# A first stage with a written order of products, and other engines for the carry weights, the latent squares and the last attention block

## The chip, the core and the metric

The kernel runs on one core of a Trainium2 chip, in one launch. A core has TensorE (PE) with its weight loads (PEld), VectorE (DVE), ScalarE (ACT), GpSimd (POOL), and SyncE (SP), which issues the transfers from the chip's main memory. Each engine runs its own list of instructions in order and waits at semaphores for the others. The metric is the device time in microseconds (us) of one execution, as the median of several runs.

## What is computed

A trunk of two layers over 512 latent tokens and 256 context tokens of width 1024, in float32. Layer 0 mixes tokens with a bidirectional mLSTM, layer 1 with windowed attention; a squared-ReLU MLP follows each. Every part is modulated by shifts, scales and gates from the condition vectors. Cut from the reference:

```
for i in range(DEPTH):                          # DEPTH = 2
    mod_l = split(silu(c) @ ada_w[i] + ada_b[i], 6)       # latent
    mod_c = split(silu(c_ctx) @ ada_w[i] + ada_b[i], 6)   # context
    u  = rms_norm(h,  norm_mix[i]) * (1 + mod_l[1]) + mod_l[0]
    uc = rms_norm(hc, norm_mix[i]) * (1 + mod_c[1]) + mod_c[0]
    y, yc = mlstm(uc, u, ...) if i == 0 else swa(uc, u, ...)
    h = h + mod_l[2] * y
    h = h + mod_l[5] * (square(relu(modulated_norm(h) @ w1)) @ w2)
    ...                                         # hc likewise, in layer 0
return rms_norm(h, final_norm)
# mlstm: q, k, v, o, gates = split(u @ w_in);  chunks of 128 tokens
#   b = cumsum(log_f);  m_t = max(max(d), b + m0);  carry_w = exp(b + m0 - m_t)
#   num = (exp(d - m_t) * (q k^T)) v + carry_w * (q C0);  h = num / max(|den|, exp(-m_t))
# swa: softmax over 384 latent keys, 256 context keys and a sink; o @ w_out
```

## The kernel before, in words

Activations lie transposed: 8 tiles (k) of 128 features, each 512 latent ("L") and 256 context ("C") tokens wide. A float32 product is made of three products of parts with fewer bits: data and weights are split into a high part (uH, whi) and a rest (uL, wlo), and `mm3` (L94 to L98) issues high by high, high by rest and rest by high. Weights come by `unit`: a load, a cast to whi on ACT (L887) and a subtraction to wlo on DVE (L888), in `split`.

The build places instructions on each engine in an order of its own, from dependencies and its estimates of durations; those marked `keep_in_program_order` (through `keep`, or through the flag `pin` in `split`) stay as written.

**First stage** (`layer0_mix`, L354 to L444). x is loaded (`load_x`); ACT squares each tile (L376), DVE adds pairs (L380), PE sums them with a ones vector (L382). DVE makes rs (L385), POOL raises it to the power -1/2 (rc, L387), PE transposes rc to rows (L321), and copies put 1/rms in rb. For each k, `cols` makes the modulation: two 512 KB tiles adaw (L204), eight products to the rows tile arow (L212), a copy on ACT, two products to fm (L221), then amix and mod on DVE (L223, L225). Per k, L417 to L420 make uH and uL for both groups, and `dense` multiplies them with three weights: m = 0 is wg (the gates), m = 1 and 2 are wqk (q and k of the first head pair). That is 8 x 3 x 2 x 3 = 144 products into the six accumulators acc.

**Gates** (`gates`). From acc of wg come scans and maxima on DVE for 8 heads in two directions, on tiles of 40 rows by 768 tokens: t1, t2, and, split in a high and a low half, ast (L652, L653) and cst (L658, L659), the carry weights; the low halves are subtracted on POOL. PE transposes t1 and t2, ACT copies them to tok1 and tok2 (L670, L675). `ogate(0, ...)` gives the output gate's products of the first head pair and is told to split its two weights on POOL. `core` of a head pair makes kp (k scaled by tok1, L764) and the carry products (L751), while a generator `fill` hands out products of the next head pair.

**End of the first MLP** (`ffn0`). `back_out` adds each output tile to hL (L1144); `norm_add` (L283 to L295) squares the finished tile on ACT and adds it to ssL. For m = 1 to 5 the add runs on POOL, for m = 6 and 7 on DVE. `keys_begin` (L1468 to L1481) then makes layer 1's key and value products (pj); between them it calls two hooks for the latent group: `norm_rc` (the sums of ssL by PE, L308, then rs and rc) after part (0, 1) of its last tile, and `norm_group` (`norm_bc`, L321, then `norm_u`, which makes layer 1's uH and uL) after part (1, 0).

**End of the attention** (`layer1_mix`, `weigh`). 16 blocks (g, j); the last product of a block leaves av; ACT copies its two halves to yt and yb (L1846, L1847), POOL adds them into yT (L1849). `split_half` splits yT for the output projection, whose last group's first half of tokens (`pa`, names "A") is laid between the blocks, and whose second half ("B") follows.

## Time and profile before

| | |
|---|---|
| runs | 1549.05, 1553.58, 1553.87 us |
| median | 1553.58 us |
| profiled execution, its own time | 1551.29 us |
| span of the profiled execution | 1549.4 us |
| mean granted TensorE clock | 0.992 |
| PE's largest group (L96 mm 128x512) | 496 products, 189.4 us |

The span runs from the first to the last instruction in the trace; the profiled execution's time contains it. "L382 <- DVE sq L380: 7.4, 1, 7.4" reads: PE at L382 waited for the tile sq, made by DVE at L380; 7.4 us in all, once, the longest 7.4. A row of the timeline has the start, the duration, engine, line, operation, tiles and shapes, and in brackets the wait that ended at its start. A row of the windows has the stretch, its length, PE's busy time and products, the granted clock (1.00 is full), the busy share of the DMA engines, and GB/s.

### The profile page before, as it was taken

The numbers are of one execution on the slowest core, as the hardware profiler recorded it, in microseconds if no ns is written. First come the engines' busy times: TensorE is split into PE (matmuls) and PEld (weight loads), VectorE is DVE, ScalarE is ACT, GpSimd is POOL, SyncE is SP. The second block draws the span as 40 slices with busy tenths as digits, with TensorE's granted clock in tenths as the row PEclk, the third lists the DMA queues.
The fourth block names the chain that finished last, engine by engine and source line by source line (L and its number), as shares of the span: only waits on it lengthen the run. The fifth ranks groups of instructions, "written<-read, shape, count | busy, mean of one in ns | idle before, by whom it ended". The sixth has DMA issues, their size and how long they took to land.

```text
span 1549.4 us, 23838 instructions
## 1 busy us (share of the span) xinstructions
PE 1509.6 (97%) x9110; PEld 1355.9 (88%) x9110; DVE 1127.1 (73%) x2084; ACT 740.2 (48%) x1501; POOL 326.5 (21%) x318
## 2 busy tenths in 40 slices
PE   6999999999999999999999999999999999999998
PEld 4778888878889999999999999888887988888886
DVE  3684657488797888767676667778888875757697
ACT  4533343344573332524424355666666665545454
POOL 0322111113203222232224221243443100000000
PEclk8999999999999999999999999999999999999999
DMA  8422323234231343343443422011111424150321
GB/s 316 139 83 69 125 82 118 73 116 150 74 110 42 120 139 124 125 146 125 148 145 100 150 69 66 32 34 42 42 41 43 177 83 149 41 163 28 109 69 55
DMA packets 47848, 157.27 MB, mean 102 GB/s; under 512 B 5327, under 2 KB 8911, under 8 KB 47607
## 3 DMA queue, kind: packets, MB, share of 16 engines
q1 hardware_dynamic: 46560, 154.25, 30.3%
q8 instruction: 72, 1.18, 0.3%
q10 hardware_dynamic: 1175, 1.51, 0.3%
q14 instruction: 41, 0.34, 0.1%
HBM read 153.64 MB, written 2.10 MB: 101 GB/s over the span
## 4 chain that ended last, share of the span: by engine, by line
PE 79%; DVE 6%; issue 4%; ACT 4%; POOL 3%; DMA 1%; POOLq 0%; DVEq 0%; ACTq 0%
PE mm L96 17%; PE mm L97 16%; PE mm L98 16%; PE p L98 2%; PE p L97 2%; PE p L96 2%; PE pt L1825 2%; PE pj L96 1%; PE pj L97 1%; PE pj L98 1%; PE at L843 1%; DVE adap L262 1%; PE av L1840 1%; ACT whi L887 1%; DVE wlo L888 1%
## 5 line engine op out<-in xcount | busy, mean ns | idle before, releaser
L888 DVE TENSOR_TENSOR wlo<-raw,whi 128x1024 fp32r<-128x1024 f32 (+2 forms) x152 | 179.6, 1186 | 82.3 <-ACT whi L887 80.6
L887 ACT CAST whi<-raw 128x1024 fp32r<-128x1024 f32 (+2 forms) x155 | 154.0, 999 | 141.9 <-PE mm L97 77.4
L96 PE MATMUL mm<-uH,whi 128*128 128x512 f32 (+1 forms) x496 | 189.4, 386 | 0.0
L97 PE MATMUL mm<-uL,whi 128*128 128x512 f32 (+1 forms) x496 | 186.7, 378 | 0.7 <-DVE uL L332 0.4
L98 PE MATMUL mm<-uH,wlo 128*128 128x512 f32 (+1 forms) x496 | 186.9, 378 | 0.0
L262 DVE SCALAR_TENSOR_TENSOR adap<-raw,crow 128x1024 bf16<-128x1024 f32 x128 | 165.8, 1295 | 19.9 <-DMA raw<-ada 19.1
L96 PE MATMUL mm<-h,whi 128*128 128x384 f32 x512 | 172.9, 338 | 1.9 <-ACT h L887 1.9
L97 PE MATMUL mm<-h,whi 128*128 128x384 f32 x512 | 172.6, 337 | 0.5 <-DVE h L888 0.5
L98 PE MATMUL mm<-h,wlo 128*128 128x384 f32 x512 | 172.1, 336 | 0.0
L887 ACT CAST whi<-sum 128x512 fp32r<-128x512 f32 (+1 forms) x42 | 31.9, 761 | 165.8 <-PE mm L97 75.9
L98 PEld LDWEIGHTS mm<-uH,wlo 128*128 128x128 f32 x496 | 93.4, 188 | 17.9 <-issue 0.9
L97 PEld LDWEIGHTS mm<-uL,whi 128*128 128x128 f32 x496 | 93.6, 189 | 16.4 <-DVE uL L489 0.7
L96 PEld LDWEIGHTS mm<-uH,whi 128*128 128x128 f32 x496 | 92.9, 189 | 15.6 <-issue 0.3
L96 PEld LDWEIGHTS mm<-h,whi 128*128 128x128 f32 x512 | 96.1, 188 | 2.8 <-ACT h L887 2.8
L97 PEld LDWEIGHTS mm<-h,whi 128*128 128x128 f32 x512 | 96.1, 188 | 1.5 <-DVE h L888 1.4
L98 PEld LDWEIGHTS mm<-h,wlo 128*128 128x128 f32 x512 | 96.1, 188 | 0.0
L888 DVE TENSOR_TENSOR wlo<-wb,whi 128x1024 fp32r<-128x1024 f32 x49 | 59.2, 1221 | 35.9 <-ACT whi L887 35.8
L888 DVE TENSOR_TENSOR h<-r,h 128x384 fp32r<-128x384 f32 (+2 forms) x100 | 56.4, 568 | 34.1 <-ACT h L887 33.8
L887 ACT CAST whi<-wb 128x1024 fp32r<-128x1024 f32 x49 | 51.6, 1054 | 60.9 <-PE mm L97 27.1
L1809 POOL TENSOR_SCALAR e<-e,den 128x512 f32<-128x512 f32 (+1 forms) x64 | 49.0, 779 | 135.1 <-DVE den L1807 86.9
L98 PE MATMUL p<-t,wlo 128*128 128x384 f32 x224 | 75.4, 337 | 0.5 <-DVE wlo L888 0.5
L97 PE MATMUL p<-t,whi 128*128 128x384 f32 x224 | 75.2, 336 | 0.0
(401 smaller groups left out, 4180.0 us busy)
## 6 DMA issues: line engine op xcount, KB each, us to landing
raw<-ada SPq DMA_DIRECT2D x80, 512.0 KB, 3.6
raw<-w SPq DMA_DIRECT2D x64, 512.0 KB, 3.5
raw<-w2a SPq DMA_DIRECT2D x32, 512.0 KB, 3.5
wb<-w2b SPq DMA_DIRECT2D x28, 512.0 KB, 4.2
adaw<-ada SPq DMA_DIRECT2D x16, 512.0 KB, 7.7
hL<-xT SPq DMA_DIRECT2D x16, 256.0 KB, 3.5
raw<-wqk SPq DMA_DIRECT2D x8, 512.0 KB, 4.0
raw<-wv SPq DMA_DIRECT2D x8, 512.0 KB, 3.5
```

The lines of the kernel that those rows point to most:

```text
L96: mm(out=out, lhsT=ah, rhs=bh, start=start, stop=False)
L97: mm(out=out, lhsT=ah, rhs=bl, start=False, stop=False)
L98: mm(out=out, lhsT=al, rhs=bh, start=False, stop=stop)
L262: self.tc.keep_in_program_order(nc.vector.scalar_tensor_tensor(out=pr, in0=w, scalar=0.5, in1=self.crow[:, v, :], op0=ALU.mult, op1=ALU.mu ...
L843: mm(out=o[hh][:, i * VW:(i + 1) * VW], lhsT=pw[g, d, hh][:, i, :], rhs=v[:, 3 * g + i, hh, :], start=False, stop=i == 2)
L887: keep(self.nc.scalar.copy(out=hi, in_=src))
L888: keep((eng or self.nc.vector).tensor_tensor(out=lo, in0=src, in1=hi.bitcast(F32), op=ALU.subtract))
L1809: nc.gpsimd.tensor_scalar(out=out[ii][:, :W], in0=out[ii][:, :W], scalar1=den[:, ii:ii + 1], scalar2=1.0, op0=ALU.mult, op1=ALU.mult)
L1825: nc.tensor.transpose(out=pt[:, i * P:(i + 1) * P], in_=ps_[i][:, n * P:(n + 1) * P], identity=self.ident)
L1840: mm(out=o, lhsT=vv, rhs=ph, start=n == 0, stop=False)
```

## The change

`mm3`, `ada_rows` and `ada_cols` issue their products through a new `matmul`, which keeps the written order while `pin_mm` is set. In the first stage it is set, and the order is written out: the modulation is cut into `rows` (eight products and the copy) and `cols` (two products and the DVE rows), the splits of wg and the first wqk stand ahead of the norm, the third split after the first products of k = 1, and wg is loaded ahead of the first adaw pair. Every second context square is made by DVE. In the gates, DVE takes the subtraction of cst's low half and the splits of the first output gate's weights; the splits of the first step of the core are pinned. In `back_out` the adds of latent tiles 4 and 5 move from POOL to DVE; the hooks of `keys_begin` move to the parts (0, 3) and (1, 1), and the sums of `norm_rc` are pinned there. In the last attention block yb's copy and both adds run on DVE, and the last three parts of `pa` are issued after the second `split_half` instead of ahead of the last products.

```diff
@@ -92,10 +92,15 @@
     def mm3(self, out, ah, al, bh, bl, start, stop):
-        mm = self.nc.tensor.matmul
+        mm = self.matmul
...
         mm(out=out, lhsT=al, rhs=bh, start=False, stop=stop)
+    def matmul(self, **kw):
+        i = self.nc.tensor.matmul(**kw)
+        return self.tc.keep_in_program_order(i) if self.pin_mm else i
@@ -209,17 +214,15 @@
             for c in range(4):
-                self.nc.tensor.matmul(out=ps[32 * c:32 * c + 32], lhsT=self.cond[:, 4 * hf + c, :],
-                                      rhs=ws[hf][:, c * 256:(c + 1) * 256], start=hf == 0, stop=hf == 1)
-    def ada_cols(self, pool, ps, fm, i):
+                self.matmul(out=ps[32 * c:32 * c + 32], lhsT=self.cond[:, 4 * hf + c, :],
+                            rhs=ws[hf][:, c * 256:(c + 1) * 256], start=hf == 0, stop=hf == 1)
+    def ada_cols(self, rows, fm, i):
...
         nc = self.nc
-        rows = pool.tile([P, 256], F32, name="rows", tag="rows", bufs=2)
-        nc.scalar.copy(out=rows, in_=ps)
         for s in range(2):
-            nc.tensor.matmul(out=fm[:, 4 * i + 2 * s:4 * i + 2 * s + 2], lhsT=rows[:, s * P:(s + 1) * P], rhs=self.sel,
-                             start=True, stop=True)
+            self.matmul(out=fm[:, 4 * i + 2 * s:4 * i + 2 * s + 2], lhsT=rows[:, s * P:(s + 1) * P], rhs=self.sel,
+                        start=True, stop=True)
@@ -367,20 +370,55 @@
             self.load_x(g)
-        aw = [self.ada_load(pool, 0)]
+        raw, w = [], []
+        def load(i):
+            r = self.ring.tile([P, D], F32, name="raw", tag="raw", bufs=self.nraw)
+            n = srcs[i].shape[1]
+            nc.sync.dma_start(out=r[:, :n], in_=srcs[i])
+            raw.append(r[:, :n])
+        def parts(i):
+            w.append([self.ring.tile([P, D], F32R, name=t, tag=t, bufs=self.nsplit)[:, :raw[i].shape[1]]
+                      for t in ("whi", "wlo")])
+            self.pin = True
+            self.split(raw[i], *w[i])
+            self.pin = False
+        aw = []
+        for i in range(3):
+            load(i)
+            aw += [self.ada_load(pool, j) for j in ((0,), (1, 2), (3,))[i]]
...
         ps = self.at.tile([P, 512], F32, name="at", tag="at")
+        self.pin_mm = True
...
                 sq = pool.tile([P, n], F32, name="sq0", tag=f"sq{g}", bufs=4)
-                nc.scalar.activation(out=sq, in_=hs[kt], func=AF.Square)
+                if g == "C" and kt % 2:
+                    nc.vector.tensor_tensor(out=sq, in0=hs[kt], in1=hs[kt], op=ALU.mult)
+                else:
+                    nc.scalar.activation(out=sq, in_=hs[kt], func=AF.Square)
...
                 for j in range(n // P):
-                    nc.tensor.matmul(out=ps[:, j0 + j:j0 + j + 1], lhsT=sq[:, j * P:(j + 1) * P], rhs=self.ones,
-                                     start=kt == 1 and j0 + j == 0, stop=kt == KT - 1 and j0 + j == NCH - 1)
+                    self.matmul(out=ps[:, j0 + j:j0 + j + 1], lhsT=sq[:, j * P:(j + 1) * P], rhs=self.ones,
+                                start=kt == 1 and j0 + j == 0, stop=kt == KT - 1 and j0 + j == NCH - 1)
+        parts(0)
+        parts(1)
+        fm = self.at.tile([P, 512], F32, name="fm", tag="at")
+        rws = {}
+        def rows(i):
+            ps = self.at.tile([P, 512], F32, name="arow", tag="at")[:, :256]
+            self.ada_rows(ps, aw[i])
+            rws[i] = pool.tile([P, 256], F32, name="rows", tag="rows", bufs=2)
+            nc.scalar.copy(out=rws[i], in_=ps)
+        def cols(i):
+            self.ada_cols(rws.pop(i), fm, i)
+        rows(0)
@@ -388,29 +426,11 @@
             (nc.vector.tensor_copy if j0 else nc.scalar.copy)(out=rb[g], in_=bc)
-        fm = self.at.tile([P, 512], F32, name="fm", tag="at")
...
         acc["C"] = [c0[:, :NCX], c12[:, :NCX], c12[:, NCX:]]
-        w = []
-        def cols(i):
-            ps = self.at.tile([P, 512], F32, name="arow", tag="at")[:, :256]
-            self.ada_rows(ps, aw[i])
-            self.ada_cols(pool, ps, fm, i)
-        def dense(g, m, k):
-            sl = slice(k * P, (k + 1) * P)
-            alone = g == "L" or m == 0
-            self.mm3(acc[g][m], w[m][0][:, sl], w[m][1][:, sl], *xs[g](k), k == 0 and (alone or m == 1),
-                     k == KT - 1 and (alone or m == 2))
-        cols(0)
-        for i in range(1, 3):
-            w.append(self.unit(srcs[i - 1]))
-            aw.append(self.ada_load(pool, i))
-            cols(i)
-        w.append(self.unit(srcs[2]))
-        for i in range(KT):
+        def modulate(i):
@@ -419,12 +439,43 @@
                                                op1=ALU.subtract)
-            if i + 3 < KT:
-                aw.append(self.ada_load(pool, i + 3))
-                cols(i + 3)
-            for m in range(3):
+        def dense(k, *ms):
+            sl = slice(k * P, (k + 1) * P)
+            for m in ms:
                 for g in "CL":
-                    dense(g, m, i)
+                    alone = g == "L" or m == 0
+                    self.mm3(acc[g][m], w[m][0][:, sl], w[m][1][:, sl], *xs[g](k), k == 0 and (alone or m == 1),
+                             k == KT - 1 and (alone or m == 2))
+        cols(0)
+        modulate(0)
+        rows(1)
+        dense(0, 0)
+        cols(1)
+        modulate(1)
+        dense(0, 1)
+        rows(2)
+        dense(1, 0)
+        parts(2)
+        cols(2)
+        modulate(2)
+        dense(1, 1)
+        dense(0, 2)
+        rows(3)
+        dense(1, 2)
+        cols(3)
+        modulate(3)
+        for i in range(2, KT):
+            if i + 2 < KT:
+                aw += [self.ada_load(pool, j) for j in range(len(aw), min(KT, i + 4))]
+                rows(i + 2)
+            dense(i, 0, 1)
+            if i + 2 < KT:
+                cols(i + 2)
+                modulate(i + 2)
+            dense(i, 2)
+        self.pin_mm = False
@@ -446,11 +497,14 @@
             self.new_es(0)
-            so = self.ogate(0, xs, nc.gpsimd)
+            so = self.ogate(0, xs, nc.vector)
...
                 pass
+            self.pin = True
+            next(so)
+            self.pin = False
@@ -465,9 +519,11 @@
                         fill = self.out_early(yu)
-                    for n in core:
+                    for i, n in enumerate(core):
+                        self.pin = p + i == 0
...
                             next(fill, None)
+                    self.pin = False
@@ -656,7 +712,7 @@
             cp(out=cst[R], in_=az)
-            nc.gpsimd.tensor_tensor(out=cst[64:104], in0=az, in1=cst[R].bitcast(F32), op=ALU.subtract)
+            nc.vector.tensor_tensor(out=cst[64:104], in0=az, in1=cst[R].bitcast(F32), op=ALU.subtract)
@@ -1145,7 +1201,7 @@
                 g = "LC"[t]
-                self.norm_add(self.st, g, m, self.hview(g, m), nc.vector if m > 5 else None)
+                self.norm_add(self.st, g, m, self.hview(g, m), nc.vector if m > (5 if t else 3) else None)
@@ -1475,7 +1531,7 @@
                     self.proj_part(self.wkv[pr], j, self.rows_of(u), 256, i, t[:, 256 * pr:256 * pr + 256])
-                    if j == 4 and (pr, i) in ((0, 1), (1, 0)):
+                    if j == 4 and (pr, i) in ((0, 3), (1, 1)):
@@ -1603,7 +1659,7 @@
                         pa = self.out_part(3, ys, pt, "pt", "A", st3)
-                        parts = [f for i in range(4) for f in (parts[i], pa[i])] + pa[4:]
+                        parts = [f for i in range(4) for f in (parts[i], pa[i])] + pa[4:5]
@@ -1612,7 +1668,10 @@
                             pass
-            self.split_half(ys[3], y3, 1)
+                self.split_half(ys[3], y3, 1)
+                for f in pa[5:]:
+                    for _ in f():
+                        pass
@@ -1843,10 +1902,11 @@
             yb = sw.tile([DH, 512], F32, name="yb", tag="sp", bufs=4)
+            last = g * 4 + j == 15
             nc.scalar.copy(out=yt, in_=o[0:DH, :])
-            nc.scalar.copy(out=yb, in_=o[DH:P, :])
+            (nc.vector.tensor_copy if last else nc.scalar.copy)(out=yb, in_=o[DH:P, :])
             for i in range(2):
-                nc.gpsimd.tensor_tensor(out=ys[g][i * DH:(i + 1) * DH, :, j * P:(j + 1) * P],
+                (nc.vector if last else nc.gpsimd).tensor_tensor(out=ys[g][i * DH:(i + 1) * DH, :, j * P:(j + 1) * P],
@@ -1873,7 +1933,7 @@
             rc, st = [], self.st
-            return [lambda: rc.append(self.norm_rc(st, g)),
+            return [lambda: rc.append(self.norm_rc(st, g, tc.keep_in_program_order)),
```

PE's list in the first stage, before, from the transposes of rc on; arow and fm are the modulation's tiles, sm and rows the copied row, acc the accumulators:

```order
L321 MATMUL at<-ident,rc_232 128x128 x6
L212 MATMUL arow<-adaw,cond 32x256 x8
L221 MATMUL fm<-sm,rows 128x2 x2
L212 MATMUL arow<-adaw,cond 32x256 x4
L96 MATMUL acc<-uH_112,whi 128x512
L212 MATMUL arow<-adaw,cond 32x256 x4
L97 MATMUL acc<-uL_113,whi 128x512
L98 MATMUL acc<-uH_112,wlo 128x512
L221 MATMUL fm<-sm,rows 128x2 x2
```

The same place after the change; all these products now go through the helper's line L102:

```order
L102 MATMUL arow<-adaw,cond 32x256 x4
L324 MATMUL at<-ident,rc_270 128x128 x6
L102 MATMUL arow<-adaw,cond 32x256 x4
L102 MATMUL fm<-sm,rows 128x2 x2
L102 MATMUL arow<-adaw,cond 32x256 x8
L102 MATMUL acc<-uC_104,whi 128x256 x2
L102 MATMUL acc<-uC_104,wlo 128x256
L102 MATMUL acc<-uH_112,whi 128x512
L102 MATMUL acc<-uL_113,whi 128x512
L102 MATMUL acc<-uH_112,wlo 128x512
L102 MATMUL fm<-sm,rows 128x2 x2
```

Half of the first arow now stands ahead of the transposes, and the second arow whole, not in two halves around a latent product, ahead of the first products, which begin with those of the context (uC).

DVE's list in the gates, before, from the cast of ast's high half to kp; ast and cst are the split pairs, adap a sum of modulation rows for later layers:

```order
L652 CAST ast<-aa 40x768
L656 TENSOR_TENSOR b<-aa,m_661 40x768
L661 TENSOR_TENSOR aa<-t_658,ae 40x768
L658 CAST cst<-b 40x768
L888 TENSOR_TENSOR wlo<-raw,whi 128x1024
L262 SCALAR_TENSOR_TENSOR adap,mod_81<-raw,crow 128x1024 x2
L888 TENSOR_TENSOR wlo<-raw,whi 128x1024
L764 TENSOR_TENSOR kp<-at,tok_646 128x384 x4
```

The same place after:

```order
L708 CAST ast<-aa 40x768
L712 TENSOR_TENSOR b<-aa,m_661 40x768
L717 TENSOR_TENSOR aa<-t_658,ae 40x768
L714 CAST cst<-b 40x768
L715 TENSOR_TENSOR cst<-b,cst 40x768
L944 TENSOR_TENSOR wlo<-raw,whi 128x1024
L820 TENSOR_TENSOR kp<-at,tok_646 128x384 x4
```

The subtraction of cst and one split of an output gate weight now stand between cst's cast and kp; the two adap rows and a second split have left.

DVE's list at the end of the first MLP, before; hL is the latent stream, uC the context's modulated tile, wlo the rest of a weight, rs what follows PE's sums of ssL:

```order
L1144 SCALAR_TENSOR_TENSOR hL_3522<-mm,mod_81,hL_3522 128x384
L888 TENSOR_TENSOR wlo<-raw,whi 128x1024
L1144 SCALAR_TENSOR_TENSOR hL_4110<-mm,mod_81,hL_4110 128x384
L1144 SCALAR_TENSOR_TENSOR hL_4121<-mm,mod_81,hL_4121 128x384
L888 TENSOR_TENSOR wlo<-raw,whi 128x1024
L295 TENSOR_TENSOR ssL<-ssL,sq 128x512 x2
L311 TENSOR_SCALAR rs<-at 128x4
```

The same place after:

```order
L298 TENSOR_TENSOR ssL<-ssL,sq 128x512
L1200 SCALAR_TENSOR_TENSOR hL_3522<-mm,mod_81,hL_3522 128x384
L944 TENSOR_TENSOR wlo<-raw,whi 128x1024
L1200 SCALAR_TENSOR_TENSOR hL_4110<-mm,mod_81,hL_4110 128x384
L298 TENSOR_TENSOR ssL<-ssL,sq 128x512
L1200 SCALAR_TENSOR_TENSOR hL_4121<-mm,mod_81,hL_4121 128x384
L298 TENSOR_TENSOR ssL<-ssL,sq 128x512
L944 TENSOR_TENSOR wlo<-raw,whi 128x1024
L298 TENSOR_TENSOR ssL<-ssL,sq 128x512
L314 TENSOR_SCALAR rs<-at 128x4
```

Two more adds to ssL stand on DVE, and the second split shown, which stood ahead of both adds, now stands behind three of the four.

More of the change, by code (lines that the diff above doesn't have):

```diff
@@ L63, in __init__ @@
         self.ada_cap = None
-        self.pin = False
+        self.pin = self.pin_mm = False
         self.ada_due = 0.0
```

## The prediction

> **What bounds the kernel now.** The page comes first: the PE row and the span.
>
> ```profile
> span 1549.4 us, 23838 instructions
> PE 1509.6 (97%) x9110; PEld 1355.9 (88%) x9110; DVE 1127.1 (73%) x2084; ACT 740.2 (48%) x1501; POOL 326.5 (21%) x318
> ```
>
> PE is idle for 1549.4 - 1509.6 = 39.8 us. A change that removes no product can win from that idle time, from products run at a low granted clock, and from nothing else. The list of what PE waited for says where the idle time lies.
>
> ```profile
> PE at L382 <- DVE sq L380: 7.4, 1, 7.4
> PE at L308 <- DVE ssL L295: 2.1, 1, 2.1
> PE acc L96 <- ACT uH L419: 2.0, 2, 1.7
> PE mm L96 <- ACT y L1655: 2.0, 1, 2.0
> PE at L751 <- DVE kp L764: 1.8, 2, 1.1
> PE at L751 <- ACT tok L670: 1.7, 1, 1.7
> ```
>
> The first row is the load of x and stays. The other five are in the four places that the diff touches: the first stage (L419), the gates' start of the mLSTM (L670, L764), the latent squares at the end of the first MLP (L295), and the end of the attention (L1655). The table of windows then shows the granted clock (the column after PE busy) at two of them.
>
> ```profile
> 23.20:26.54 3.34, 1.18 (x13) 0.98 1.02 408
> 26.54:36.70 10.16, 9.92 (x41) 0.50 0.75 280
> 36.70:70.00 33.30, 33.12 (x236) 1.00 0.36 128
> 940.60:948.00 7.40, 7.11 (x35) 0.54 0.16 65
> ```
>
> After a thin stretch (1.18 us of work in 3.34) the first stage runs 10.2 us at half clock, then 33.3 us at full clock without idle time, up to its last product. The same follows the stall before 940.54. So an idle microsecond in these two places costs more than itself.
>
> The profiled execution took 1551.29 us, 1.9 more than its span; the sum goes against it. The three timed runs have their median 2.3 above it (1549.05 to 1553.87).
>
> **First stage.** Nothing is removed; it is an order. The rows that set it:
>
> ```profile
> 18.32 1.35 POOL L387 TENSOR_TENSOR rc<-rs,mhalf 128x6 f32<-128x6 f32 x1 [15.09 <-DVE rs L385]
> 21.19 1.94 PE L212 MATMUL arow<-adaw,cond 128*32 128x256 f32 x16
> 24.26 0.28 DVE L223 TENSOR_SCALAR amix<-fm,ab,sm 128x2 f32<-128x2 f32 x1 [3.40 <-PE fm L221]
> 27.18 0.74 DVE L420 SCALAR_TENSOR_TENSOR uL<-hL,mod,uH 128x512 fp32r<-128x512 f32 x1
> 35.64 0.63 PE L98 MATMUL acc<-uH,wlo 128*128 128x512 f32 x1
> 36.07 0.63 PE L97 MATMUL acc<-uL,whi 128*128 128x512 f32 x1
> 43.42 0.39 PE L96 MATMUL acc<-uH,whi 128*128 128x512 f32 x1
> 43.66 0.39 PE L97 MATMUL acc<-uL,whi 128*128 128x512 f32 x1
> 44.12 0.28 PE L96 MATMUL acc<-uC,whi 128*128 128x256 f32 x1
> 44.24 0.27 PE L97 MATMUL acc<-uC,whi 128*128 128x256 f32 x1
> 44.44 0.64 PE L212 MATMUL arow<-adaw,cond 128*32 128x256 f32 x8
> 45.01 0.38 PE L98 MATMUL acc<-uC,wlo 128*128 128x256 f32 x1
> ```
>
> From start to start, a 512-wide product takes 0.24 us (43.42 to 43.66; at half clock 0.43, 35.64 to 36.07) and a 256-wide one 0.12, so the six products of one (k, m) take 1.06. Half an arow takes 0.57 (44.44 to 45.01); with the slower product behind it I reckon 1.33 for a whole one, and 0.48 for the fm pair. Both are estimates; they are checked on the old stage: of its 144 products 133 remain at 36.70 (the 41 rows of the window are 24 of arow, 6 of fm and 11 products), 61 of them wide: 14.6 + 72 x 0.12 = 23.3, and five arow in halves (1.52) with fm 10.0, together 33.3 as measured.
>
> The new order from the same rows. Half of arow 0 moves into the wait for POOL's rc, so the second half alone stands behind the transposes: 1.0 earlier; the squares now shared with DVE give 0.1, as PE's own cold products pace them. The first amix comes at 23.2 instead of 24.26. The chain amix to the end of uL keeps its length, 27.92 - 24.26 = 3.66: uL ends at 26.9. arow 1 stands whole ahead of the first products (23.2 to 24.3) instead of in two halves around one that waits until 26.54. The last two wide products of (0, 0) follow uL at half clock, to 27.7; fm 1 to 28.3 (estimated at somewhat over its 0.48), the six of (0, 1) to 30.2. If the clock is back by then, the rest is arow 2 1.33, (1, 0) 1.06, fm 2 0.48, (1, 1) 1.06: 34.1. Then (0, 2) waits for the third weight's low half, which DVE now makes inside modulate(2): about 35.1, its last products 35.9. arow 3 and (1, 2) reach 38.3; fm 3, four more arow and fm, and six k of 3.18 are 26.8: the stage ends at 65.1 instead of 70.0. One window more at half clock (3.4 us) takes back 1.7. I take **4.5**. The bounds: 1.0 (two windows more, and a wait for loads) and 6.5 (never cold).
>
> The loads are the cover that could go. wg is now issued ahead of ada's first pair.
>
> ```profile
> 10.73 0.91 SPq L204 DMA_DIRECT2D adaw<-ada  x2
> adaw<-ada SPq DMA_DIRECT2D x2, 512.0 KB, 5.6
> ```
>
> The two loads of that pair, issued from 10.73 on, landed 5.6 later on the median, so the first at about 16.3. With one 512 KB load ahead, 1.3 us at the 408 GB/s of the window's row, it lands at 17.6; PE wants it when its last square sum is done, a little before rc's start at 18.32. If it is late, the transposes behind it in PE's queue are late with it, by 1.3 at most; that is within the lower bound.
>
> **Gates.** DVE instead of POOL subtracts cst (L659) and splits the first head pair's wo.
>
> ```profile
> 77.29 0.95 DVE L625 SCALAR_TENSOR_TENSOR gz<-gz,aa 40x768 f32<-40x768 f32 x1 [3.94 <-ACT aa L623]
> 88.09 0.55 DVE L652 CAST ast<-aa 40x768 fp32r<-40x768 f32 x1
> 91.29 3.18 POOL L888 TENSOR_TENSOR wlo<-raw,whi 128x1024 fp32r<-128x1024 f32 x1
> 92.12 2.76 DVE L658 CAST cst<-b 40x768 fp32r<-40x768 f32 x1
> 95.03 2.79 POOL L659 TENSOR_TENSOR cst<-b,cst 40x768 fp32r<-40x768 f32 x1 [0.56 <-DVE cst L658]
> 101.23 1.94 DVE L764 TENSOR_TENSOR kp<-at,tok 128x384 f32<-128x384 f32 x4
> ```
>
> The cast of cst takes 2.76 beside POOL's split and 0.55 alone. Then the cast ends at about 92.7 and the subtraction (0.95, as the 40x768 of L625) at 93.6 instead of 97.82. The Trainium skill, "SBUF — State Buffer", section "Who interferes with whom", has the two engines share a port pair by a lock, so that the second waits until the first is done; the cast did end 0.4 behind the split (94.88 against 94.47), so the trace agrees, and it gives the sum nothing further.
>
> Two of the splits now on DVE (1.26 each, as the row 937.83 below has a split alone) fit into the 3.94 before gz. The third stands before the kp rows: queued behind it are kp, then PE's fourth carry product. With tok copied ahead of the casts on ACT, the split ends at about 100.0, and kp starts there instead of 101.23 (two adap rows have left its way). The wait for tok (1.7) goes, and of the wait for kp the smaller of its two times, 1.8 - 1.1 = 0.7; the longer lies at a later head pair. The sum is 2.4; I take **2.0**, bounds 0.5 (a third split that comes late) and 2.4.
>
> **Latent squares.** For m = 4 and 5 the add moves from POOL to DVE, and the sum's products go behind nine more pj products.
>
> ```profile
> 934.48 3.52 POOL L295 TENSOR_TENSOR ssL<-ssL,sq 128x512 f32<-128x512 f32 x2 [2.86 <-ACT sq L291]
> 934.85 2.00 DVE L888 TENSOR_TENSOR wlo<-raw,whi 128x1024 fp32r<-128x1024 f32 x1
> 937.83 1.26 DVE L888 TENSOR_TENSOR wlo<-raw,whi 128x1024 fp32r<-128x1024 f32 x1
> 939.01 1.47 DVE L295 TENSOR_TENSOR ssL<-ssL,sq 128x512 f32<-128x512 f32 x2
> 940.54 1.28 PE L308 MATMUL at<-ones,ssL 128*128 128x1 f32 x8 [2.05 <-DVE ssL L295]
> ```
>
> DVE was the engine that came last here, not POOL: POOL was done at 938.0, DVE's last add at 940.48. DVE gets two adds more (2 x 0.74 = 1.5) and one split is 0.8 shorter, so its last add ends about 0.7 **later**, at 941.2, and the last split, now behind three of the four adds, at 940.6. PE then stalls for that split and again for the sum, some 2 us as before, but with nine products (1.1) more behind it. Net 0.3 to 1.1 if the clock falls as before. The half-clock stretch (7.4 us, 46% lost, 3.4 us) may stay out, since the stall falls into other windows. I take **0.8**; bounds -1.0 (the last split later still) and 3.0 (no half clock, less a wait that then shows in the uL chain).
>
> The Trainium skill, "TensorE: Matmul & The Clock Gate", section "Why this matters for your kernels", wants PE's gaps below about 3 us for the clock to stay. By that rule a stall of 2.05 us would cost only itself and this term would be 0.8 with no upper end; the 0.54 of the window's row speaks against it.
>
> **End of the attention.**
>
> ```profile
> 1193.98 0.58 ACT L1846 COPY yt<-av 64x512 f32<-64x512 f32 x1 [0.41 <-PE av L1841]
> 1194.58 0.58 ACT L1847 COPY yb<-av 64x512 f32<-64x512 f32 x1
> 1195.24 1.58 POOL L1849 TENSOR_TENSOR yT<-yt,yb 64x256 f32<-64x256 f32 x2 [0.77 <-ACT yb L1847]
> ```
>
> From the last av product to y's cast (L1655) there are two copies, then two adds on POOL. On two engines the copies lie side by side (0.6 less). The adds on DVE have no row here; they lie between 0.74 for both (an add twice as wide takes 0.74, the row at 939.01) and POOL's 1.58, and I take 0.8, as DVE's row is the nearer one: 0.8 less. That is 1.4 of a wait of 2.0. The last av products also move six narrow products (0.7) ahead, which adds to the cover; against it two DVE rows (nAuH, hL) now stand before y's low half, and DVE may still be at one when yb is wanted, some 0.5 each at most. I take **1.2**, bounds 0.6 and 2.0.
>
> **Sum.** 4.5 + 2.0 + 0.8 + 1.2 = 8.5: 1551.3 - 8.5 = 1542.8. Placing it halfway from the profiled run to the median adds 1.2: **1544.0**.
>
> **Rivals.**
> - *The clock comes back early*: full clock in the first stage from the start and no half-clock stretch at the squares: 6.5 + 2.0 + 3.0 + 1.2 = 12.7, so 1539.8. For it: the written order has no gap of several us. Against: the first products still wait for uL.
> - *The first stage's gain is given back*: the gates' chain (DVE scans, ACT's tables) starts from the same products, but if a load or the crow rows hold it, PE waits where it did not. Then 4.0 is left: 1548.5. Against: DVE had 3.94 to spare before gz, more than the two splits that are put there.
> - *The change does little*: the lower bounds of all four, 1.1 in sum, 1551.4.
> - *The written order keeps PE cold*: pinned products cannot pass a waiting one, so each wait thins its window; if none fills up before the stage ends, 35 us of work take about 1.8 times as long (a wide product 0.43 against 0.24), 28 more, of which the terms give back 8: 1571. It decides at the share of the window that PE streams; 33.3 to 36.7 was enough before.
>
> **How the numbers follow.** Forecast 0.55, early clock 0.18, gain given back 0.12, little 0.11, cold 0.04. What a measurement of this kernel can tell from no change is about 0.3%, 4.7 us, so faster means below 1548.9: 0.55 + 0.18 and half of the third, 0.79; slower 0.04; same 0.17. The range takes the sum of the bounds, 13.9 and 1.1: 1537.5 to 1550.5, and leaves out the cold case and some of the little one.
>
> **What would show it.** Right: the first stage's last product at 64 to 67 us; no PE wait for tok; the row of L295 before the sum's products still on DVE, at about 2 us; the wait for y below 0.8. Wrong: half clock in the windows beyond 33 us, a PE wait for adaw before 20 us, or the gates' transposes waiting for ACT.

## The result, and the profile after

The changed kernel took 1542.54 us in the median (5 runs, 1542.0 to 1546.33); the kernel before 1553.58 (5 runs, 1549.05 to 1556.65). The ratio is 0.9941, with a 95% interval of 0.9920 to 0.9961. The profiled execution has a span of 1540.2 us, 9.2 less than before.

The page of the changed kernel: the span and the busy times, then, from the list of what PE waited for, the rows that answer to the six of before, and the new ones. All products of `mm3` now have the line L102.

```profile
span 1540.2 us, 23828 instructions
PE 1505.4 (98%) x9110; PEld 1354.4 (88%) x9110; DVE 1130.9 (73%) x2097; ACT 739.1 (48%) x1496; POOL 313.4 (20%) x310
...
PE at L102 <- DVE sq L404: 6.6, 2, 6.4
...
PE pj L102 <- DVE wlo L944: 1.7, 2, 1.3
...
PE at L807 <- DVE kp L820: 1.2, 1, 1.2
PE mm L102 <- ACT y L1714: 1.0, 1, 1.0
PE mm L102 <- DVE wlo L944: 0.9, 1, 0.9
...
PE acc L102 <- DVE uC L440: 0.7, 1, 0.7
```

The waits for tok and for the sum of ssL are gone, the wait for y is halved. New are 0.9 for a weight's low half (mm) and 1.3 of the 1.7 for another (pj). PE's idle time fell from 39.8 to 34.8 us and its busy time by 4.2, with the same 9110 products. So somewhat over half of the gain is idle time; the rest is the same products in less busy time, most of it at the keys, where a stretch at half pace is gone.

To see where, both traces are cut at the same instructions. Of the changed kernel's timeline (start, duration, engine, line, operation): the end of the square sums, the last product of the first stage, the first carry product of the second head pair, the first and the last key product of the context, the last row of a query's transposes, and the first sum of the output's second half.

```profile
16.86 0.56 PE L102 MATMUL at<-ones,sq 128*128 128x1 f32 x2
66.31 0.39 PE L102 MATMUL acc<-uH,wlo 128*128 128x512 f32 x1
173.84 0.77 PE L807 MATMUL at<-cst,es 104*128 104x384 f32 x3
927.61 0.28 PE L102 MATMUL pj<-whi,uC 128*128 128x256 f32 x1
943.49 0.28 PE L102 MATMUL pj<-whi,uC 128*128 128x256 f32 x1
1157.45 0.45 PE L1809 MATMUL pt<-identr,qsp 128*128 128x128 f32 x3
1198.44 0.61 PE L311 MATMUL at<-ones,ssB 128*128 128x1 f32 x4 [0.42 <-DVE ssB L298]
```

The stretches between these points (starts, of the first row the end), with the same points of every other trace of this study. "Between" is everything from the second head pair to the keys, "attention" from the keys' end to the last query:

| kernel | start | stage | gates | between | keys | attention | end | rest | span |
|---|---|---|---|---|---|---|---|---|---|
| before | 18.03 | 52.00 | 109.16 | 754.17 | 19.04 | 213.55 | 41.49 | 341.96 | 1549.4 |
| after | 17.42 | 48.89 | 107.53 | 753.77 | 15.88 | 213.96 | 40.99 | 341.76 | 1540.2 |
| e1_first_back | 17.99 | 50.57 | 106.38 | 752.98 | 15.89 | 213.45 | 41.02 | 341.82 | 1540.1 |
| e2_gates_back | 18.63 | 49.63 | 116.73 | 752.86 | 17.39 | 213.42 | 40.76 | 341.98 | 1551.4 |
| e3_squares_back | 18.05 | 47.61 | 107.53 | 752.44 | 19.11 | 213.84 | 40.74 | 341.78 | 1541.1 |
| e4_end_back | 17.96 | 49.72 | 107.52 | 757.95 | 15.89 | 213.75 | 41.50 | 341.71 | 1546.0 |
| e5_spare | 17.89 | 45.71 | 107.54 | 752.74 | 15.89 | 213.88 | 40.98 | 341.77 | 1536.4 |
| e6_splits | 17.57 | 43.31 | 107.52 | 753.67 | 15.89 | 213.82 | 41.00 | 341.82 | 1534.6 |
| e7_both | 18.30 | 42.39 | 107.52 | 752.95 | 15.89 | 213.84 | 41.00 | 341.81 | 1533.7 |
| e8_rst | 18.07 | 48.84 | 106.37 | 757.35 | 18.25 | 213.89 | 40.69 | 341.74 | 1545.2 |
| e9_late_pool | 17.28 | 45.92 | 107.52 | 752.80 | 14.99 | 217.81 | 40.74 | 341.74 | 1538.8 |
| e10_early_dve | 18.35 | 46.98 | 107.54 | 754.26 | 18.92 | 213.88 | 41.02 | 341.75 | 1542.7 |
| e11_best | 17.88 | 42.17 | 106.36 | 755.47 | 15.89 | 213.97 | 40.71 | 341.75 | 1534.2 |
| e12_best2 | 18.00 | 43.07 | 106.37 | 754.02 | 15.89 | 213.96 | 40.71 | 341.78 | 1533.8 |

Between the two profiled executions the stage gave 3.1, the gates 1.6, the keys (where the latent squares stand) 3.2, the end 0.5: 8.4 of 9.2. The columns also show how far one trace of a kernel may be read. Where the order is the same and the clock holds, gates and keys agree to 0.02 us from trace to trace; the stage and "between" scatter by 2 us and more. (The 0.6 by which the start differs is scatter too: the four other traces of this written order have 18.0 to 18.6.)

### The profile page after: what moved, and what is told of

Read it like the earlier page. It is cut to its first block, busy times and chain, and to the rows that moved or that the text cites. A ratio compares the mean times of both kernels' runs of the same rounds, so it can differ in the third digit from the quotient of the medians.

```text
span 1540.2 us, 23828 instructions
## 1 busy us (share of the span) xinstructions
PE 1505.4 (98%) x9110; PEld 1354.4 (88%) x9110; DVE 1130.9 (73%) x2097; ACT 739.1 (48%) x1496; POOL 313.4 (20%) x310
## 4 chain that ended last, share of the span: by engine, by line
PE 78%; DVE 7%; issue 5%; ACT 4%; POOL 4%; DMA 1%; POOLq 0%; ACTq 0%; DVEq 0%
PE mm L102 50%; PE p L102 5%; PE pj L102 4%; PE kept L102 2%; PE pt L1884 2%; DVE adap L265 1%; PE acc L102 1%; PE at L899 1%; ACT whi L943 1%; PE av L1899 1%; DVE wlo L944 1%; PE pb L102 1%; PE pc L102 1%; PE av L1900 1%; PE at L862 1%
## 5 line engine op out<-in xcount | busy, mean ns | idle before, releaser
L102 PE MATMUL mm<-h,whi 128*128 128x384 f32 x1024 | 264.8, 339 | 2.2 <-ACT h L943 1.7
L944 DVE TENSOR_TENSOR wlo<-raw,whi 128x1024 fp32r<-128x1024 f32 (+2 forms) x155 | 183.6, 1188 | 86.9 <-ACT whi L943 86.1
L102 PEld LDWEIGHTS mm<-h,whi 128*128 128x128 f32 x1024 | 186.4, 189 | 4.1 <-ACT h L943 2.6
L102 PE MATMUL mm<-uH,whi 128*128 128x512 f32 (+1 forms) x496 | 189.2, 386 | 0.3 <-ACT uH L334 0.3
L102 PE MATMUL mm<-uL,whi 128*128 128x512 f32 (+1 forms) x496 | 186.8, 378 | 0.8 <-DVE uL L335 0.4
L102 PE MATMUL mm<-uH,wlo 128*128 128x512 f32 (+1 forms) x496 | 187.0, 378 | 0.0
L102 PE MATMUL mm<-h,wlo 128*128 128x384 f32 x512 | 172.6, 337 | 0.0
L102 PE MATMUL p<-t,whi 128*128 128x384 f32 x448 | 114.3, 336 | 0.0
L102 PEld LDWEIGHTS mm<-uH,wlo 128*128 128x128 f32 x496 | 93.4, 188 | 17.9 <-issue 0.9
L102 PEld LDWEIGHTS mm<-uL,whi 128*128 128x128 f32 x496 | 93.6, 189 | 16.3 <-DVE uL L545 0.7
L102 PEld LDWEIGHTS mm<-uH,whi 128*128 128x128 f32 x496 | 92.9, 189 | 16.0 <-ACT uH L334 0.5
L102 PEld LDWEIGHTS mm<-h,wlo 128*128 128x128 f32 x512 | 96.7, 189 | 0.0
L102 PEld LDWEIGHTS p<-t,whi 128*128 128x128 f32 x448 | 81.3, 188 | 0.0
L102 PE MATMUL mm<-uC,whi 128*128 128x256 f32 x416 | 78.2, 288 | 0.3 <-ACT whi L943 0.3
L102 PE MATMUL p<-t,wlo 128*128 128x384 f32 x224 | 75.4, 337 | 0.2 <-DVE wlo L944 0.2
```

Of the source, the lines that this page charges most:

```text
L102: i = self.nc.tensor.matmul(**kw)
L944: keep((eng or self.nc.vector).tensor_tensor(out=lo, in0=src, in1=hi.bitcast(F32), op=ALU.subtract))
```

## The experiments

Four kernels undo one place each. (The numbers of the table are the readings; the medians of their runs scatter as widely as what is asked. The kernel before, timed beside these kernels, had a median of 1552.38 beside e1 to e4, 1550.01 beside e5 to e8 and 1554.91 beside e9 to e12, so a difference of 2 us between medians of different groups says nothing.)

**e1_first_back**: the first stage as before, the rest changed.

```diff
-        cols(0)
-        modulate(0)
-        rows(1)
-        dense(0, 0)
...
+        cols(0)
+        for i in range(1, 3):
+            w.append(self.unit(srcs[i - 1]))
+            aw.append(self.ada_load(pool, i))
+            cols(i)
...
```

> The changed kernel with the first stage as it was before; the other three places keep the change. As the milestones of the two traces read, the written order is worth 3.3 us up to the stage's last product (70.0 against 66.7): 1545.8, and the last product of the stage ends near 70. As predicted, 4.5: 1547.0. If the gain of the first stage is given back behind it, and the gates set the time anyway: 1542.5 to 1543.5, with a PE wait in the gates gone.

1543.44 us (7 runs, 1542.14 to 1549.57): only 0.9 above the changed kernel. The stage took 50.57, the old order's second trace after 52.00; five traces of the written order have 47.6 to 49.7, in the mean 48.94. So the order is worth 51.29 - 48.94 = 2.35 in the stage, from two traces against five. But the gates took 106.38 here and 107.53 with the written stage: 1.15 of it is given back at once. The net is 1.2, which the medians can't tell from nothing. The give-back stands in the changed kernel's timeline, on POOL, ACT's queue, ACT, DVE and PE:

```profile
65.08 0.74 POOL L670 MEMSET t<- 104x768 f32 x1
65.85 0.29 ACTq L671 DMA_DIRECT2D t<-cst  x1
66.56 1.05 ACT L943 CAST whi<-raw 128x1024 fp32r<-128x1024 f32 x1 [4.11 <-POOL m L670]
67.64 1.46 DVE L944 TENSOR_TENSOR wlo<-raw,whi 128x1024 fp32r<-128x1024 f32 x1 [1.26 <-ACT whi L943]
69.15 0.39 PE L102 MATMUL mm<-wlo,uC 128*128 128x256 f32 x1 [0.90 <-DVE wlo L944]
```

POOL clears the gates' tile t, ACT's queue issues a load into t behind that, and the cast of wv's second unit stands behind the load in the same queue. With the stage's end 3 us earlier, this chain, which starts at POOL no earlier than before, is what comes late.

**e8_rst** tests that: POOL's masks and its clearing of ast and cst stand behind the clearing of t and the load into it.

```diff
-        nc.gpsimd.tensor_copy(out=self.idb, in_=ident)
...
-        nc.gpsimd.memset(ast.bitcast(F32), 0.0)
-        nc.gpsimd.memset(cst.bitcast(F32), 0.0)
...
             nc.scalar.dma_start(out=rst, in_=a["cst"][0:40, C_RST:C_RST + T])
...
+            nc.gpsimd.tensor_copy(out=self.idb, in_=ident)
...
+            nc.gpsimd.memset(ast.bitcast(F32), 0.0)
+            nc.gpsimd.memset(cst.bitcast(F32), 0.0)
```

> The changed kernel with POOL's clearing of the gates' tile t1 ahead of its masks, so that the load into it, which waits in ACT's queue ahead of the cast of wv's second unit, is issued some 3 us earlier. If PE's new wait of 0.9 for that unit's low half is due to this queue, it falls to 0 to 0.3, and the stretch from the stage's last product to the first kp product (33.4 us in four traces of the changed kernel's order) takes 32.3 to 32.6: 1541.6. If the cast waits for its buffer instead, nothing changes: 1542.5, 33.4.

The load was issued at 62.07, PE's wait is gone, and the gates took 106.37. Its time, 1543.86 (6 runs, 1540.68 to 1547.03), doesn't show it: against the changed kernel's trace this one has 3.6 more in "between" and 2.4 more at the keys, where the clock fell.

**e2_gates_back**: cst's low half and the two splits on POOL, no pins.

```diff
-            nc.vector.tensor_tensor(out=cst[64:104], in0=az, in1=cst[R].bitcast(F32), op=ALU.subtract)
+            nc.gpsimd.tensor_tensor(out=cst[64:104], in0=az, in1=cst[R].bitcast(F32), op=ALU.subtract)
...
-            so = self.ogate(0, xs, nc.vector)
+            so = self.ogate(0, xs, nc.gpsimd)
...
-            self.pin = True
-            next(so)
-            self.pin = False
```

> The changed kernel with POOL again at the low half of cst and at the two splits of the first output gate, and no pinned splits there. Prediction and milestones agree on 2.0: 1544.5, with PE waiting about 1.7 us for tok near 95 us again. The milestones put 0.7 of it up to the first kp and 1.3 between 117 and 337 us; if that 1.3 has another cause, only 0.7 comes back: 1543.2, and the lead over the kernel before still grows by 1.3 between those points.

1546.03 us (12 runs, 1544.06 to 1553.31): 3.5 more. With the old stage, old gates take 109.16 and new ones 106.38 (e1): 2.8. Half of it, 1.4, lies ahead of the first kp; the other half behind, up to the second head pair, where PE has 104 wide products in place of 110: one step of the output gate, six products of 0.235, now stands ahead of kp and fills the wait. In this trace the place cost 9.2: behind the stall the clock fell. Its timeline and its windows (stretch, length, PE, PEld, DVE, ACT, POOL busy, clock, DMA share, GB/s):

```profile
100.07 0.59 PE L802 MATMUL at<-cst,es 104*128 104x384 f32 x2 [2.57 <-ACT tok L721]
...
100.00:113.00 13.00, 12.45 (x50) 8.20 (x51) 8.88 (x18) 2.50 (x11) 0.40 (x1) 0.56 0.25 82
```

**e3_squares_back**: the adds of m = 4 and 5 on POOL, the old hooks, no pin.

```diff
-                self.norm_add(self.st, g, m, self.hview(g, m), nc.vector if m > (5 if t else 3) else None)
+                self.norm_add(self.st, g, m, self.hview(g, m), nc.vector if m > 5 else None)
...
-                    if j == 4 and (pr, i) in ((0, 3), (1, 1)):
+                    if j == 4 and (pr, i) in ((0, 1), (1, 0)):
...
-            return [lambda: rc.append(self.norm_rc(st, g, tc.keep_in_program_order)),
+            return [lambda: rc.append(self.norm_rc(st, g)),
```

> The changed kernel with the latent adds of m = 4 and 5 on POOL, the hooks after the parts (0, 1) and (1, 0), and the sums not pinned. If the place is worth 3.1 by its own order (the stall in front of the sum, 2.05 us, thins one clock window, and two run at half speed): 1545.6, with a half-clock stretch of some 7 us behind the sum in the trace. If the order itself is worth 0.8, as predicted, and the rest was where the stall fell among the windows: 1543.3, and no half-clock stretch there, or one only in some runs.

1543.26 us (6 runs, 1541.76 to 1547.9), which alone would speak for 0.8. The trace speaks for 3.2: the keys took 19.11, as before the change, with the same stall and the same fall of the clock:

```profile
932.81 1.87 PE L311 MATMUL at<-ones,ssL 128*128 128x1 f32 x8 [2.05 <-DVE ssL L298]
...
932.80:940.20 7.40, 7.09 (x34) 6.80 (x35) 3.04 (x6) 1.38 (x2) 1.83 (x5) 0.54 0.15 60
```

That its median was not 3.2 higher is within the scatter: the kernel had the shortest "between" of all (752.44), and six runs are few.

What in the edit does it? The lists of instructions answer one part: with the hooks and the pin undone but the adds on DVE, every engine's list is row for row that of the changed kernel; with the adds undone alone it is row for row that of e3. So the moved hooks and the pin do nothing; the build moved the sums behind more key products because of the adds. Two kernels with pinned key products part the adds from the place of the sums. (They also pin the transposes of rc, which alters their first stage; only the keys are read.)

```diff
+        self.pin_mm = True
         for j in (4, 5):
...
-                    if j == 4 and (pr, i) in ((0, 3), (1, 1)):
-                        hooks[pr]()
+                    if (j, pr, i) in ((4, 1, 3), (5, 0, 0)):
+                        hooks[(j, pr, i) == (5, 0, 0)]()
```

**e9_late_pool** has this and the adds on POOL; **e10_early_dve** keeps the adds on DVE and calls the hooks at (4, 1, 1) and (4, 1, 2).

> The changed kernel with the adds of m = 4 and 5 on POOL again, but with the key products pinned so that the sums of ssL stand behind 48 of them (about where they stand after the change, not behind 36). If the place of the sums on PE is what keeps the clock up, the stretch from the first key product to the last one of the context stays at 15.9 us (as in six traces with the change). If the adds on DVE do it: 19.1, as in both traces without them, with a half-clock stretch.

> The other way round: the adds of m = 4 and 5 on DVE as after the change, the sums pinned behind 36 key products as before. If the place of the sums decides: 18.5 to 19.5 us for the same stretch, PE stalls 2 us or more in front of the sums, and the clock falls behind them. If the adds on DVE decide: 15.9 to 16.5.

The sums in the two timelines, e9 and then e10, and e10's window behind them:

```profile
930.71 1.04 PE L311 MATMUL at<-ones,ssL 128*128 128x1 f32 x8
```

```profile
934.60 1.87 PE L311 MATMUL at<-ones,ssL 128*128 128x1 f32 x8 [2.42 <-DVE ssL L298]
...
934.60:942.60 8.00, 8.00 (x43) 7.84 (x44) 3.65 (x7) 1.38 (x2) 1.83 (x5) 0.61 0.20 68
```

The place of the sums decides, by one trace of each. Behind 48 products they wait for nothing and the clock stays, even with POOL's adds (15.0); behind 36 PE stalls 2.4 and falls to half pace, even with DVE's (18.9). The place is no full proof against the clock: e9 lost 3.9 later, in "attention" (waits of 0.9 for ksp, 1.5 for qsp and 0.8 for qs, then a clock of 0.60 near 964). The medians, 1542.55 (4 runs, 1540.65 to 1546.3) and 1544.36 (5, 1541.37 to 1545.44), don't tell the two apart: both stand at 0.9927 of the kernel before.

**e4_end_back**: the last attention block as before.

```diff
-            (nc.vector.tensor_copy if last else nc.scalar.copy)(out=yb, in_=o[DH:P, :])
+            nc.scalar.copy(out=yb, in_=o[DH:P, :])
...
-                (nc.vector if last else nc.gpsimd).tensor_tensor(out=ys[g][i * DH:(i + 1) * DH, :, j * P:(j + 1) * P],
+                nc.gpsimd.tensor_tensor(out=ys[g][i * DH:(i + 1) * DH, :, j * P:(j + 1) * P],
...
-                        parts = [f for i in range(4) for f in (parts[i], pa[i])] + pa[4:5]
+                        parts = [f for i in range(4) for f in (parts[i], pa[i])] + pa[4:]
```

> The changed kernel with the last attention block as it was before (ACT and POOL at the halves and adds, the last parts ahead of the last products). As predicted, 1.2: 1543.7, PE waits 2.0 for y. As the milestones read, 0.1 to 0.7: 1542.6 to 1543.2; the wait for y is then longer again by 1.0, and something else behind it absorbs part of it.

1545.57 us (8 runs, 1540.75 to 1552.33), of which the place has little: the end took 41.50, as before, against 40.69 to 41.02 in the traces with the change, 0.6 in the mean. The rest of its 1546.0 lies in "between" (757.95), where PE fell to half pace near 323, 422 and 651 us.

Three kernels ask why the written stage took 48.9 and not 45.

**e5_spare**: eleven products whose result is thrown away, in three waits of the stage.

```diff
+        def spare(n):
+            for _ in range(n):
+                self.matmul(out=acc["L"][2], lhsT=w[0][0][:, 0:P], rhs=w[0][0][:, 0:512], start=True, stop=True)
...
+        spare(3)
         dense(0, 0)
```

> The changed kernel with eleven spare products (128x512, into an accumulator that is started anew later) in three waits of the first stage: six ahead of the transposes of rc, two ahead of the first fm, three ahead of the first product of uC. In the four traces of the written order the products from fm (about 23.5 us) to 32 to 36 us come at half pace, 0.43 us a wide product. If the pace follows from how much PE had streamed shortly before, it stays at 0.24, and the stage from the first arow product to its last product takes 45 to 46.5 us in place of 47.7 to 49.8: about 1539.5. If the half pace there has another cause (time since the start, the loads at 400 GB/s), the spare products change nothing or cost: 48 to 50, 1542 to 1544.

1540.22 us (5 runs, 1537.11 to 1542.48), and the stage 45.71, with more work in it. (The edit also writes out the order of the first modulated tiles. By it DVE makes the third split earlier, and PE's wait of 0.6 for it is gone; that is part of the 3.2 by which the stage is shorter.) The timelines show the pace: the last square sums, half an arow and two wide products of the changed kernel, and then two wide products of e5.

```profile
15.55 1.87 PE L102 MATMUL at<-ones,sq 128*128 128x1 f32 x8 [0.19 <-DVE sq L404]
17.36 1.08 PE L102 MATMUL arow<-adaw,cond 128*32 128x256 f32 x8
...
28.20 0.63 PE L102 MATMUL acc<-uL,whi 128*128 128x512 f32 x1
28.63 0.63 PE L102 MATMUL acc<-uH,wlo 128*128 128x512 f32 x1
```

```profile
29.87 0.40 PE L102 MATMUL acc<-uH,whi 128*128 128x512 f32 x1
30.10 0.40 PE L102 MATMUL acc<-uL,whi 128*128 128x512 f32 x1
```

A wide product follows the one before it after 0.43 without the spare products, after 0.23 with them. The half pace was there earlier: eight square sums took 1.87, where the eight sums of ssL at 935.17 take 0.95, and half an arow took 1.08, where at full pace it takes 0.64. So PE had not fallen to half pace, it had not yet left it. The changed kernel's trace has its first record of the clock at 33.9 us, and there the pace rises to full; in the four other traces of this order that is at 31.7 to 36.8, in e5 at 23.1. So the pace follows what PE did shortly before. The time since the start isn't it, for the rise moved by 8.6 us and more, and neither are the loads, which in e5 ran at 404 to 415 GB/s from 21 to 30 us.

The Trainium skill, "TensorE: Matmul & The Clock Gate", section "Why this matters for your kernels", has the throughput drop after idle gaps above about 3 us. The written stage can't test that, as its pace had not come up. The kernel before can: its pace came up at 23.0 and fell at 26.4, beside a wait of 1.74 that was the longest since the rise, so the trace doesn't agree:

```profile
26.54 0.79 PE L96 MATMUL acc<-uH,whi 128*128 128x512 f32 x1 [1.74 <-ACT uH L419]
```

**e6_splits**: DVE's splits out of the way, and the transposes behind all of the first arow.

```diff
-        parts(0)
-        parts(1)
+        parts(0, lo=False)
+        parts(1, lo=False)
...
+            tc.keep_in_program_order((nc.vector.tensor_copy if j0 else nc.scalar.copy)(out=rb[g], in_=bc))
+        parts(0, hi=False)
...
         modulate(0)
+        parts(1, hi=False)
...
         modulate(1)
+        parts(2)
...
-        parts(2)
```

> The changed kernel with another written order: DVE's subtraction for wg's low half behind the rstd copy, not beside POOL's rc; that of the first wqk behind the first uL; all eight arow products and then the transposes. If rc takes 2.26 because DVE works beside it, it takes 1.35 again, and the first uC comes 2 to 3 us earlier: the stage takes 45 to 47 instead of 47.7 to 49.8, time about 1540. If rc's 2.26 had another cause, rc stays, and only the order of uC is gained: 46.5 to 48.5, 1541.5.

1536.99 us (4 runs, 1536.36 to 1537.35); the stage took 43.31, better than either theory. Three things changed at once and are not told apart: rc, the split that stood between hL and uC on DVE (from amix to the end of uL 3.0 in place of 3.7), and the pace, which came up at 25.1 without any spare product. POOL's rc in the changed kernel and in e6:

```profile
17.71 2.26 POOL L425 TENSOR_TENSOR rc<-rs,mhalf 128x6 f32<-128x6 f32 x1 [14.49 <-DVE rs L423]
```

```profile
17.85 1.35 POOL L429 TENSOR_TENSOR rc<-rs,mhalf 128x6 f32<-128x6 f32 x1 [14.59 <-DVE rs L427]
```

Alone it takes 1.35, beside DVE's split 2.26 (2.27 in e5, which leaves that split in place); all fourteen traces have one or the other. The Trainium skill, "SBUF — State Buffer", section "Who interferes with whom", has a DVE instruction with two inputs in SBUF contend with a POOL instruction that reads there; the 0.91 agree.

**e7_both** adds four spare products ahead of the first product of uC; **e11_best** adds e8's clearing to it, and **e12_best2** is e6 with that clearing.

> The kernel of the run before with four spare products ahead of the first product of uC. If the clock follows PE's load: full pace throughout, the stage takes 44 to 45, time about 1538.5. If not: as the run before, or 0.5 longer.

> The kernel of e7_both (splits moved, transposes behind all eight arow products, four spare products) with the clearing of t1 moved as in e8_rst. By the sum of the two: first stage 42.4 us, the stretch to the second head pair's carry products 106.4 instead of 107.5, so 6.5 + 1.1 less than the changed kernel: about 1535. If the earlier clearing takes back what the stage wins (POOL or ACT late somewhere), 1537 to 1539 as the two kernels without it.

> The same without the four spare products (e6_splits with the earlier clearing). First stage 43.3, the stretch behind it 106.4: about 1536. If the spare products are needed to keep the clock, some runs show a stage of 46 to 48 us, and the median is 2 to 3 above that of the run with them.

| kernel | median | runs | ratio to before |
|---|---|---|---|
| e7_both | 1539.30 | 5, 1535.44 to 1540.37 | 0.9918 (0.9900 to 0.9936) |
| e11_best | 1535.54 | 5, 1532.88 to 1536.01 | 0.9876 (0.9855 to 0.9897) |
| e12_best2 | 1540.10 | 6, 1535.54 to 1544.01 | 0.9909 (0.9885 to 0.9933) |

e7's stage was shorter than e6's, 42.39, but its median isn't: the four spare products show no gain in time. e11 beats both kernels, the one before and the changed one, by the amounts expected: stage 42.17, gates 106.36. Whether the spare products are what sets it apart from e12 stays open. In e12's own trace the pace came up at 20.8 without them (stage 43.07); its two slowest runs have no trace, but a granted clock of 0.993 against 0.997 in the fastest, so they ran at half pace more often, and where isn't known.

## Why the prediction came out as it did

The total was right, 1544.0 against 1542.54 and 8.5 against 9.2 between the profiled executions. But its four terms were 4.5, 2.0, 0.8 and 1.2, and the traces speak for 2.35 (1.2 with what is given back), 2.8, 3.2 and 0.6. Each sign is right and each size is off; that the errors cancel is luck.

- **First stage, 4.5: too much.** In the mean of the traces 2.35, and 1.2 when what follows is counted. "The first amix comes at 23.2 instead of 24.26": it came at 24.13, behind square sums that ended 0.6 earlier by scatter. The sum had taken rc at the old 1.35, but the written order puts DVE's split beside it, 0.91 more; and it had kept the old trace's two fm products, 0.61 at a pace that had just come up. Here, at half pace, they took 1.01. "uL ends at 26.9": 27.8, all of it from the late amix. The chain kept its 3.66 as said; a split stands in it between hL and uC in both kernels, here the old row and the new ones:

```profile
25.64 1.22 DVE L888 TENSOR_TENSOR wlo<-raw,whi 128x1024 fp32r<-128x1024 f32 x1
```

```profile
24.13 0.28 DVE L226 TENSOR_SCALAR amix<-fm,ab,sm 128x2 f32<-128x2 f32 x1 [2.95 <-PE fm L102]
...
25.51 1.22 DVE L944 TENSOR_TENSOR wlo<-raw,whi 128x1024 fp32r<-128x1024 f32 x1
...
27.05 0.74 DVE L440 SCALAR_TENSOR_TENSOR uL<-hL,mod,uH 128x512 fp32r<-128x512 f32 x1
```

  "If the clock is back by then", at 30.2: it was at half pace from the start and came up at 33.9, so the early end of the half pace was a hope. (The sign "half clock in the windows beyond 33 us" could not show it, as the windows have 1.00 there.) Of the 4.9 that the list gave, the prediction kept 4.5, though it priced one window more at 1.7. "About 35.1" for the third weight is 37.5. The cold rival had the mechanism right (waits thin what PE streams), and it didn't decide: the pace came up at 31.7 to 36.8.
- **What is late next: left out of the sum.** The rival of a stage gain given back named the scans, the tables, "a load or the crow rows", and would leave 4.0. It was a load, in ACT's queue behind POOL's clearing, and it took 1.15, shown by e8.
- **Gates, 2.0: right in its cause, too small.** The cast of cst took 0.55, as said, and both waits went, 1.70 and 0.67, the 2.4 that the sum had found and that the prediction shaded to 2.0. The measured 2.8, above the bound of 2.4, has 0.4 more, and that is busy time: the same products took that much less, which no term had.
- **Latent squares, 0.8: much too small**, 3.2, above the bound of 3.0. "PE then stalls for that split and again for the sum, some 2 us as before" failed: PE waited 1.34 for the split and not at all for the sum, as its list shows.

```profile
934.48 0.38 PE L102 MATMUL pj<-wlo,uC 128*128 128x256 f32 x1 [1.34 <-DVE wlo L944]
...
935.17 0.95 PE L311 MATMUL at<-ones,ssL 128*128 128x1 f32 x8
...
937.49 0.65 PE L324 MATMUL at<-ident,rc 128*128 128x128 f32 x4 [0.78 <-POOL rc L316]
```

  The idle time is about as long as before (0.33, 1.34 and 0.78 against 0.4, 2.05 and 0.3). But it comes in pieces, with products between, and the half pace that cost 3 us stays out. The prediction saw that it might and priced it at its bound; it took the value next to the other end because it read the stall's length and not its shape. In two of the ten traces with this order of the keys (e2, e8) the clock fell all the same, for 1.5 and 2.4, behind the same waits of 0.33 and 1.34.
- **End of the attention, 1.2: half of it.** The wait for y went from 1.95 to 0.95, above the 0.8 set as the mark. "On two engines the copies lie side by side (0.6 less)" failed: DVE was at another add until 1185.09, and then it started yb only when ACT's copy of yt was done; what ties the two copies together isn't shown. The adds took what was estimated for them, 0.84, but an hL row stood ahead of them, the "some 0.5 each at most" of the prediction. Here is y's cast in the kernel before, and then the five rows of the chain in the changed kernel, on ACT and DVE:

```profile
1196.86 0.71 ACT L1655 CAST y<-yT 128x256 fp32r<-128x256 f32 x2 [1.07 <-POOL yT L1849]
```

```profile
1184.77 0.58 ACT L1906 COPY yt<-av 64x512 f32<-64x512 f32 x1 [0.21 <-PE av L1900]
1185.39 0.69 DVE L1907 COPY yb<-av 64x512 f32<-64x512 f32 x1 [0.29 <-ACT yt L1906]
1186.11 0.48 DVE L1739 SCALAR_TENSOR_TENSOR hL<-mm,mod,hL 128x256 f32<-128x256 f32 x1
1186.51 0.84 DVE L1909 TENSOR_TENSOR yT<-yt,yb 64x256 f32<-64x256 f32 x2
1187.39 0.71 ACT L1714 CAST y<-yT 128x256 fp32r<-128x256 f32 x2 [0.28 <-DVE yT L1909]
```

  From yt's start (1193.98 before) to y's start the chain takes 2.62 in place of 2.88, so the other engine is worth 0.26. The rest of the 1.0 that the wait lost, some 0.7, is what the prediction gave as cover: the six narrow products that now follow the last av products. Of the 1.0, 0.6 arrived at the next fixed point; 0.28 of the rest is a new wait of PE, for uH, which the kernel before and e4 don't have:

```profile
1195.14 0.62 PE L102 MATMUL mm<-uH,whi 128*128 128x256 f32 x3 [0.28 <-ACT uH L334]
```

## What to carry to other kernels

Price a stall by its shape as well as its length: here some 2.5 us of idle time around the sums cost about 3 more with one piece of 2.05 than with none above 1.34, in eight traces of ten. When an order is written out by hand, list for each engine what now stands beside the steps of the chain, splits and queue entries too; here a split beside POOL's power took 0.9 from the new order and a load ahead of a cast 1.15. And where a few microseconds are asked of a kernel whose runs scatter by more, cut the traces at fixed instructions and compare the stretches, not the medians.

## What the runs showed of the hardware that was not expected

- Besides the first stage, PE's half pace comes at the same few places of the program and in some executions only: near 100 (e2), 320 (e4, e8), 420 (before and eight others), 645 (seven traces) and behind the sums (five). The trace without one at 420 and 645 (e3) has 752.4 us in "between", the one with most (e4) 758.0. Runs without a trace have a mean granted clock on record. In the 44 runs of the kernel before beside the experiments, 1548.76 to 1559.07 us, the seven above 1556 have 0.990 to 0.992, the mean of all is 0.993. So the half pace is a part of the scatter of the runs; that it is most of it isn't shown.
- In each trace all changes of the clock lie whole multiples of 3.41 us apart. So the same waits can lie differently on that grid from run to run, which may be why e2 and e8 fell behind the sums and eight other traces didn't; no run here moves the waits alone.
- Where the trace has no record of the clock yet, the windows show 1.00. In the changed kernel's first stage the wide products stood 0.43 us apart, the half pace, while the row says 1.00:

```profile
27.00:30.00 3.00, 2.82 (x10) 2.55 (x11) 0.85 (x3) 0.00 (x0) 0.00 (x0) 1.00 1.02 403
```

  The first record is the rise at 33.9. The distance of like products is the safer reading.
- POOL's power on 128x6 took 1.35 us alone and 2.26 beside one DVE subtraction of 1.23 us.
